# A two-layer encoder on one core: one more pair of the output projection by 7 products, two added transfers issued apart, and new numbers for the planner

## The chip, the cores and the metric

The kernel runs on one core of a Trainium2 chip. The metric is the device time of one execution in microseconds (us), the median of several runs. TensorE (PE in the profile) does the matmuls, VectorE (DVE) and ScalarE (ACT) the elementwise work, GpSimd (POOL) issues a part of the transfers and raises to powers, SyncE (SP) issues the loads of weights and the final stores.

## The reference

Two layers over 256 tokens of width 4096, all in float32. A layer normalises x, multiplies it by one combined matrix, runs grouped-query attention with axial rotary embedding and a two-way decayed retention on the parts, gates both, and adds the output projection to x:

```python
h = rmsnorm(x, norm_w[l])
proj = h @ w_in[l]                                  # 4096 x 11264
aq, ak, av, ag, rq, rk, rv, rg = jnp.split(proj, SPLIT_POINTS, axis=-1)
...
a_out = silu(ag) * gqa_attention(aq, ak, av)
r_out = silu(rg) * rmsnorm(bidirectional_retention(rq, rk, rv, ...), ret_norm[l])
x = x + jnp.concatenate([a_out, r_out], axis=-1) @ w_out[l]     # 4096 x 4096
```

A final normalisation with final_norm follows the second layer.

## The kernel before

**Blocks, pairs and products.** Each projection is computed in blocks of 2 x 512 output columns: 11 blocks of w_in and 4 blocks of w_out in each layer, 30 in all. A block sums over 4096 rows of the matrix, which are 32 tiles of 128, taken as 16 pairs (0 to 15). For one pair the work is a 2 x 2 by 2 x 2 product of tiles (two token tiles, two row tiles, two column halves). Plainly, that is 8 products of a 128 x 128 by a 128 x 512 tile. The pairs in SEVEN (0, 3, 6, 9, 12) do it with 7 products instead, after Strassen and Winograd: sums of x tiles and sums of weight tiles are made first, and seven results go into seven banks of PSUM, M1 to M7, which run over all pairs of the block. The other pairs do 8 products into four of the same banks (M2 to M5), using a third version of x (tile x3, the difference of two x tiles) so that their results fit the same final combination. In w_out the pairs in MORE take 7 products too. SEVENS holds both lists (for w_in, for w_out), EIGHTS the pairs that are in neither.

**Precision.** Every float32 value is split into a high part and a low part of the faster format float32r. A product is three matmuls: x high by weight high, x low by weight high, x high by weight low. In the profile these are the lines 1458 (high weights, two matmuls) and 1468 (low weights, one).

**Pages.** The weights of a pair come as two tiles of 128 x 2 x 512 (wraw, loaded by SP, 512 KB each) and are turned into pages, each a high part (whi, a copy on ACT) and a low part (wlo, a subtraction on DVE). A pair with 8 products has two pages, A and B, with 4 products each. A pair with 7 has four: A (M1, M3), T (M5, M7), B (M2, half a page), U (M6, M4); T and U are made of sums (wsum) that DVE computes first. RING = 5 pages are prepared ahead; a page that PE has used up lets the page five places on begin. The page B of the pairs in FAR_PAIRS (2, 5, 8, 11, 14) goes another way: ACT writes its high part and the negative of it (fhi, flo), and an adding transfer from POOL's queue makes the low part.

**Order.** GROUPS cuts the pairs into groups, each beginning with a pair of 7 products; pages_of lays the pages of the other pairs of a group between the four pages of its first pair. For w_out the groups are (0), (1,2), (3,4,5), (6,7,8), (9,10,11), (12,13,14,15). block (line 1347) makes the list of products, moves the product M7 of pair 0 to the second place, and sorts all products of pair 15 to the end in the order M3, M5, M4, M2 so that banks are finished one after another. combine (line 1475) empties a bank when its last product is issued: ACT copies M1, DVE adds the others into the tiles ca and cb (seven adds of 512 columns; M6 and M7 first).

**Last block.** Its order is M5, M2, M3, M4. The M4 products of the five pairs in DELAYED are left to the very end, so that the other banks can be finished, normalised and stored meanwhile. The halves of pages that these products need are kept in buffers of x whose pairs are done (dead_room, line 581, takes them in a fixed list). last_combine (line 1565) adds x, and finishes and stores the rows of the first token tile (row 0), then those of the second (row 1), eight stores of 256 KB each.

**Other work and the planner.** Attention, retention, the splitting of the next stage's x, and the tasks of a finished block are generators that are stepped while the program is built. The program keeps clocks of PE, DVE and ACT (Now, Clock) with assumed costs, and room (line 558) lets an optional step in only where weights would still be ready:

```python
low = 1.25 + 2 * PASS + MARGIN - rush[0]
...
max(ve.until, now.t) + STEP_V + low <= limit
and max(ac.until + STEP_S, free) + 1.05 + low <= end
```

PASS is 0.2; rush is 1.5 in the first block of w_out and 0 otherwise; limit and end are the times at which PE would reach the first page whose low part isn't issued, and the first page that isn't begun. LANDING, STORE, FETCH and FAR_LANDING are assumed times of transfers (a task that has issued one waits so long by the planner's clock before its next step). EARLY lets a task's next step come before its last operation is over. TIGHT_A and TIGHT_B are how many products at the start and the end of a block get a stricter test. The order in which instructions are issued is fixed when the program is built; on the chip the engines wait for each other by semaphores.

**After a block of w_out.** out_tasks (line 1558) adds the rows of x to the two finished tiles ca and cb by two adding transfers from POOL's queue, waits LANDING, and runs out_task for each: squares (ACT), a store of the new x, a transposition (DVE), a store or a move into place for the next layer. In the last layer it loads gains and multiplies by them instead.

## Time and profile before

| | |
|---|---|
| median of 3 runs | 2625.7 us (2624.82 to 2630.23) |
| the profiled execution, its own time | 2625.96 us |
| its span, from the first to the last instruction | 2623.8 us |
| granted TensorE clock, mean | 0.998 |
| DMA, mean over the span | 261 GB/s, of which HBM read 637.60 MB, written 44.04 MB |

How to read the rows: the engines are PE (TensorE matmuls), PEld (its weight loads, beside PE), DVE, ACT, POOL and SP; a name with q is an engine's queue of issued transfers. L1458 is line 1458 of the kernel; L247 is the helper through which all DVE and ACT operations are issued, so these are told apart by their tiles, written as out<-in. A row of a group gives the shapes, the count after x, then the busy time, the mean duration of one in ns, the idle time of the engine ahead of them, and what ended it. A row of waits gives who waited for whom: us in total, times, the longest. A row in order of time begins with the start and the duration in us; the idle time before it stands in brackets. Matmuls are pipelined: a row's duration (389 ns) is longer than the step from one to the next.

### The profile page before, as it was taken

Reading aid. Unit: us, or ns where it says so; the run is one execution under the profiler, and the core shown is the slowest. Engines: PE = TensorE matmul, PEld = TensorE weight load, DVE = VectorE, ACT = ScalarE, POOL = GpSimd, SP = SyncE. Lnnn points to the kernel's source line nnn. Section 1 sums busy time; section 2 is a strip of 40 time slices with the busy share of each in tenths; the row PEclk is TensorE's granted clock in tenths of the full one; section 3 lists DMA queues with packets and bytes.
Section 4 is the critical chain, followed back from the end, with each engine's and each line's share of the span. In section 5 each row is a group of like instructions: output and inputs, shape, how many; then the busy total and the mean of one; then the engine's idle time right before and its main releaser. Section 6 shows DMA issues by size and latency. Waiting matters only on the chain.

```text
span 2623.8 us, 34532 instructions
## 1 busy us (share of the span) xinstructions
PE 2601.0 (99%) x11725; PEld 2154.2 (82%) x11725; DVE 2166.6 (83%) x2684; ACT 1804.2 (69%) x2576; POOL 372.9 (14%) x510
## 2 busy tenths in 40 slices
PE   9999999999999999999999999999999999999998
PEld 7788888888888888888878888888888888888886
DVE  7898887798778898877978878888887688987876
ACT  8676676667565788655877666776576557876655
POOL 0012211221111101111111111211210111010000
PEclk9999999999999999999999999999999999999999
DMA  9988888887778777889988888888877787788887
GB/s 305 285 262 285 272 271 284 270 269 243 235 238 249 239 249 237 274 262 281 311 246 259 271 274 283 266 273 288 280 231 217 245 258 239 221 259 264 254 249 228
DMA packets 201121, 683.94 MB, mean 261 GB/s; under 512 B 24176, under 2 KB 30832, under 8 KB 200944
## 3 DMA queue, kind: packets, MB, share of 16 engines
q1 hardware_dynamic: 147760, 521.27, 56.3%
q0 software_dynamic: 53184, 160.46, 26.5%
q8 instruction: 92, 1.51, 0.2%
q14 instruction: 85, 0.70, 0.1%
HBM read 637.60 MB, written 44.04 MB: 260 GB/s over the span
## 4 chain that ended last, share of the span: by engine, by line
PE 92%; issue 1%; DMA 1%; ACT 1%; DVE 1%; POOL 0%; POOLq 0%; DVEq 0%; ACTq 0%
PE M L1458 59%; PE M L1468 30%; PE ps L973 1%; PE ps L974 1%; PE ps L975 1%; DMA q<-q_dram 1%; PE ps L1458 0%; DMA wraw<-in_w_in 0%; DVE wlo L247 0%; ACT ca L247 0%; DVE ca L247 0%; PE ps L1468 0%; DVE cb L247 0%; ACT pr L247 0%; ACT whi L247 0%
## 5 line engine op out<-in xcount | busy, mean ns | idle before, releaser
L247 ACT CAST whi<-wraw 128x1024 fp32r<-128x1024 f32 (+1 forms) x808 | 768.7, 962 | 463.0 <-PE M L1458 310.3
L247 DVE TENSOR_TENSOR wlo<-wraw,whi 128x1024 fp32r<-128x1024 f32 (+1 forms) x808 | 886.9, 1110 | 236.6 <-ACT whi L247 230.9
L1458 PE MATMUL M<-whi,x8h 128*128 128x512 f32 x1340 | 521.9, 389 | 0.0
L1458 PE MATMUL M<-whi,x8l 128*128 128x512 f32 x1340 | 521.5, 389 | 0.0
L1458 PE MATMUL M<-whi,x7h 128*128 128x512 f32 x1265 | 493.9, 390 | 3.7 <-DVE ca L247 2.5
L1458 PE MATMUL M<-whi,x7l 128*128 128x512 f32 x1265 | 492.9, 390 | 0.0
L247 ACT CAST whi<-wsum 128x1024 fp32r<-128x1024 f32 x314 | 329.6, 1050 | 137.1 <-PE M L1458 93.8
L1468 PE MATMUL M<-wlo,x8h 128*128 128x512 f32 x1340 | 420.2, 389 | 0.0
L247 DVE TENSOR_TENSOR wlo<-wsum,whi 128x1024 fp32r<-128x1024 f32 x314 | 382.5, 1218 | 38.7 <-ACT whi L247 36.8
L1468 PE MATMUL M<-wlo,x7h 128*128 128x512 f32 x1265 | 407.8, 389 | 1.1 <-DVE wlo L247 1.1
L1458 PEld LDWEIGHTS M<-whi,x8h 128*128 128x128 f32 x1340 | 251.6, 188 | 51.7 <-issue 0.2
L1458 PEld LDWEIGHTS M<-whi,x8l 128*128 128x128 f32 x1340 | 251.6, 188 | 51.7 <-issue 0.2
L1468 PEld LDWEIGHTS M<-wlo,x8h 128*128 128x128 f32 x1340 | 251.2, 188 | 51.7
L1458 PEld LDWEIGHTS M<-whi,x7h 128*128 128x128 f32 x1265 | 237.8, 188 | 55.7 <-DVE ca L247 2.9
L1468 PEld LDWEIGHTS M<-wlo,x7h 128*128 128x128 f32 x1265 | 237.5, 188 | 50.5 <-DVE wlo L247 1.5
L1458 PEld LDWEIGHTS M<-whi,x7l 128*128 128x128 f32 x1265 | 238.0, 188 | 48.9
L1458 PE MATMUL M<-whi,x 128*128 128x512 f32 x840 | 258.9, 389 | 0.7 <-ACT whi L247 0.7
L505 POOL DMA_DIRECT2D flo<-in_w_in x108 | 97.3, 901 | 1044.4 <-ACT flo L247 1001.4
L247 ACT CAST fhi<-wraw 128x1024 fp32r<-128x1024 f32 (+1 forms) x148 | 154.7, 1045 | 99.8 <-PE M L1458 93.9
L247 DVE TENSOR_TENSOR wsum<-wraw 128x1024 f32<-128x1024 f32 x157 | 191.2, 1218 | 18.7 <-DMA wraw<-in_w_out 11.3
L1458 PEld LDWEIGHTS M<-whi,x 128*128 128x128 f32 x840 | 157.1, 188 | 32.9 <-ACT whi L247 1.1
L1458 PE MATMUL M<-fhi,x8h 128*128 128x512 f32 x440 | 171.3, 389 | 0.0
(301 smaller groups left out, 3282.9 us busy)
## 6 DMA issues: line engine op xcount, KB each, us to landing
wraw<-in_w_in SPq DMA_DIRECT2D x700, 512.0 KB, 5.0
wraw<-in_w_out SPq DMA_DIRECT2D x256, 512.0 KB, 5.2
flo<-in_w_in POOLq DMA_DIRECT2D x108, 512.0 KB, 7.9
flo<-in_w_out POOLq DMA_DIRECT2D x38, 512.0 KB, 8.8
full<-next_dram POOLq DMA_DIRECT2D x18, 512.0 KB, 7.7
p_dram<-room POOLq DMA_DIRECT2D x64, 128.0 KB, 4.6
pT<-p_dram POOLq DMA_DIRECT2D x16, 512.0 KB, 8.1
next_dram<-room POOLq DMA_DIRECT2D x40, 128.0 KB, 5.9
```

What stands on the lines that cost most here:

```text
L247: return call(out, *args, **kwargs)
L505: nc.gpsimd.dma_start(g.lo[h], g.src[0][:, h, :], accum_op=ALU.add)
L973: nc.tensor.matmul(out, a[0], b[0], start=start, stop=False)
L974: nc.tensor.matmul(out, a[0], b[1], start=False, stop=False)
L975: nc.tensor.matmul(out, a[1], b[0], start=False, stop=stop)
L1458: nc.tensor.matmul(acc[name], a[i], g.hi[h], start=m == first[name] and not i, stop=False)
L1468: nc.tensor.matmul(acc[name], a, g.lo[h], start=False, stop=m == final[name])
```

## The change

Pair 13 joins pair 1 in MORE, so that in w_out it takes 7 products with four pages, and not 8 with two. From this follow: the groups of w_out become (0), (1,2), (3,4,5), (6,7,8), (9,10,11), (12), (13,14,15); EIGHTS has nine pairs; DELAYED becomes (8,10,11,14,15) where it was (10,11,13,14,15); one more buffer pair x7h, x7l is held, and one set of x8h, x8l, x3 less. dead_room takes its buffers in the order of the pairs instead of from a list. In out_tasks the second of the two adding transfers is issued a step of APART = 5.0 us of planner's time after the first; the first tile's task starts LANDING after the first issue as before, the second's not before LANDING after its own. Seven numbers of the planner are changed.

```diff
@@ -39,7 +39,7 @@
 RING = 5
 FAR = 1
 
-STEP_V = 1.6
+STEP_V = 0.7
 STEP_S = 1.3
 
 V_FIXED = 0.15
@@ -49,14 +49,14 @@
 PASS = 0.2
 
 LANDING = 11.0
-STORE = 8.0
-FETCH = 13.0
-FAR_LANDING = 11.0
-MARGIN = 0.0
+STORE = 6.0
+FETCH = 11.0
+FAR_LANDING = 13.0
+MARGIN = 0.6
 
 RUSH = 1.5
 
-EARLY = 0.7
+EARLY = 0.4
 
 ADD_AHEAD = 2.5
 
@@ -65,7 +65,7 @@
 PE_REST = 1.5
 
 TIGHT_A = 3
-TIGHT_B = 5
+TIGHT_B = 4
 
 AT_ONCE = 2
 
@@ -77,7 +77,7 @@
 
 SEVEN = (0, 3, 6, 9, 12)
 
-MORE = (1,)
+MORE = (1, 13)
 
 DELAYED = tuple([_p for _p in range(NP) if _p not in SEVEN + MORE][-5:])
 
@@ -211,6 +211,8 @@
 PLAIN_ORDER = ("M3", "M8", "M4", "M2")
 
 EASY = ("M7",)
+
+APART = 5.0
 
 TOGETHER = 4
 BANKS = ("M1", "M2", "M3", "M4", "M5", "M6", "M7", "M8")
@@ -589,8 +591,11 @@
                 "x7h": ("x7h", o, [P, 7, P], "p k t -> p (k t)"),
                 "x7l": ("x7l", o, [P, 7, P], "p k t -> p (k t)"),
             }
-            order = "x7h x7l x3 x3 x7h x7l x7h x7l x3 x8h x8l x7h x7l x3 x8h x8l x7h x7l x3 x7h" if MORE else "x3 x3 x8h x8l x3 x3 x8h x8l x7l x7h x3 x3 x8h x8l x3 x3 x8h x8l x7l x7h"
-            rooms.extend(kinds[v] for v in order.split())
+            for p in range(NP):
+                if p not in EIGHTS:
+                    rooms.extend(kinds[v] for v in ("x7h", "x7l"))
+                else:
+                    rooms.extend(kinds[v] for v in ("x3", "x8h", "x8l")[: 3 if p in EIGHTS[2:] and p not in DELAYED else 1])
         tag, bufs, shape, flat = rooms.pop(0)
         return t(ap, shape, tag, bufs, F32R).rearrange(flat)[:, :NB]
 
@@ -1558,9 +1563,13 @@
     def out_tasks(l, n, c):
         for i in range(2):
             nc.gpsimd.dma_start(c[i], residual(l, 2 * n + i), accum_op=ALU.add)
-        yield LANDING
-        for i in range(2):
-            yield from out_task(l, 2 * n + i, c[i])
+            if i < 1:
+                yield APART
+        second = now.t + LANDING
+        yield max(0.0, LANDING - APART)
+        yield from out_task(l, 2 * n, c[0])
+        yield max(0.0, second - now.t)
+        yield from out_task(l, 2 * n + 1, c[1])
 
     def last_combine(res):
```

## The prediction

> **What bounds the kernel now.** I read the page first (busy times, then the waits of TensorE), then the w_out stage block by block, because that is where the change removes work.
>
> ```profile
> span 2623.8 us, 34532 instructions
> ...
> PE 2601.0 (99%) x11725; PEld 2154.2 (82%) x11725; DVE 2166.6 (83%) x2684; ACT 1804.2 (69%) x2576; POOL 372.9 (14%) x510
> ...
> PE M L1468 <- DVE wlo L247: 2.8, 2, 1.7
> PE M L1458 <- DVE ca L247: 2.5, 3, 1.0
> PE ps L973 <- ACT pr L247: 2.0, 2, 1.0
> PE M L1458 <- DVE cb L247: 1.2, 1, 1.2
> PE ps L1671 <- DVE junk L247: 1.1, 1, 1.1
> PE M L1458 <- ACT whi L247: 0.7, 1, 0.7
> PE M L1452 <- ACT full L247: 0.7, 1, 0.7
> ```
>
> PE (TensorE) is busy 99% of the span, and all its listed waits together come to 11.0 us. The kernel is a queue of matmuls with almost no holes; time goes down by as many matmuls as are taken out, and up by any hole that is made. The row with junk and the one with full are the start, which the change leaves alone; 9.2 us of waits lie in the body.
>
> The blocks of w_out (one block is 1024 output columns), from windows cut where one block's first matmul starts to the next one's; columns are length, then busy time and instructions of PE, PEld, DVE, ACT, POOL, the granted clock, DMA share and GB/s:
>
> ```profile
> 978.30:1064.40 86.10, 86.10 (x392) 71.55 (x391) 77.43 (x104) 70.01 (x112) 8.14 (x8) 1.00 0.74 231
> ...
> 1230.40:1313.40 83.00, 83.00 (x367) 68.73 (x367) 76.95 (x111) 69.18 (x114) 14.66 (x21) 1.00 0.92 302
> ...
> 2363.30:2446.30 83.00, 83.00 (x368) 68.72 (x367) 64.50 (x68) 50.51 (x59) 6.09 (x7) 1.00 0.85 260
> ```
>
> DVE is the second engine: 77.43 of 86.10 us in layer 0's first w_out block, 76.95 of 83.00 in its last, but only 64.50 of 83.00 in a quiet one. So the cover for new DVE work is 6 to 18 us a block.
>
> **The change, part by part.**
>
> *Pair 13 with 7 products.* A product is three matmuls. Eight blocks of w_out (four in each layer) lose one product each: 8 x 3 = 24 matmuls. One step of the queue, from rows of single matmuls near the end (twelve steps between the last two of these):
>
> ```profile
> 2598.84 0.62 PE L1468 MATMUL M<-wlo,x7h 128*128 128x512 f32 x2
> ...
> 2609.27 0.39 PE L1468 MATMUL M<-x7h,x8h 128*128 128x512 f32 x1
> ...
> 2611.99 0.39 PE L1468 MATMUL M<-x7h,x8h 128*128 128x512 f32 x1
> ```
>
> (2611.99 - 2609.27) / 12 = 0.2267 us, so 24 x 0.2267 = 5.44 us leave the queue. That is the one sure term: **-5.44**.
>
> What it adds is weight preparation:
>
> ```profile
> L247 DVE TENSOR_TENSOR wlo<-wraw,whi 128x1024 fp32r<-128x1024 f32 x643 | 781.9, 1219 | 226.5 <-ACT whi L247 221.3 <-PE M L1458 2.4 <-PE M L1468 0.9
> ...
> L247 DVE TENSOR_TENSOR wlo<-wsum,whi 128x1024 fp32r<-128x1024 f32 x314 | 382.5, 1218 | 38.7 <-ACT whi L247 36.8 <-PE M L1468 1.5
> L247 ACT CAST whi<-wsum 128x1024 fp32r<-128x1024 f32 x314 | 329.6, 1050 | 137.1 <-PE M L1458 93.8 <-DVE wsum L247 37.0 <-PE M L1468 5.1
> ...
> L247 DVE TENSOR_TENSOR wsum<-wraw 128x1024 f32<-128x1024 f32 x157 | 191.2, 1218 | 18.7 <-DMA wraw<-in_w_out 11.3 <-DMA wraw<-in_w_in 7.4
> ...
> L247 DVE TENSOR_TENSOR wlo<-wraw,whi 128x512 fp32r<-128x512 f32 x165 | 113.0, 685 | 10.1 <-ACT whi L247 9.6 <-issue 0.2
> L247 DVE TENSOR_TENSOR wsum<-wsum,wraw 128x512 f32<-128x512 f32 x157 | 108.7, 692 | 5.5
> L247 DVE TENSOR_TENSOR wsum<-wraw,wsum 128x512 f32<-128x512 f32 x157 | 107.4, 684 | 0.1
> L247 ACT CAST whi<-wraw 128x512 fp32r<-128x512 f32 x165 | 102.0, 618 | 54.1 <-PE M L1458 46.9 <-DMA wraw<-in_w_out 6.7 <-ACT x L247 0.5
> ```
>
> A pair with 7 products costs DVE its sums (1.22 + 0.69 + 0.68) and the low parts of four pages (1.22, 1.22, 0.69, 1.22): 6.94 us. A pair with 8 costs two low parts, 2.44. So DVE gets 4.50 us more in each block, ACT 3 x 1.05 + 0.62 - 2 x 1.05 = 1.67 us. The same two weight tiles are loaded, so no DMA is added. In the quiet block DVE goes to 69.0 of 82.3 us: hidden. In layer 0's first block it is 81.9 of 85.4, in its last 81.5 of 82.3: hidden only if nothing is out of place. The added work of splitting x for pair 13 (once per layer) is a few DVE operations under 1 us and goes with this.
>
> *The order at the end of a block.* The groups were (12,13,14,15) and become (12) and (13,14,15). Products of pair 15 are sorted to the end, so the bank M6 used to get its last product in 12's page U, then came 14's page B (12 matmuls) and pair 15 (24 matmuls): 36 x 0.2267 = 8.16 us to the next block. Now it gets it in 13's page U, with only pair 15 behind it: 5.44 us. DVE therefore has 2.72 us less for the adds that empty the banks before the next block writes into them. The last 8.2 us of layer 0's four blocks:
>
> ```profile
> 1056.10:1064.40 8.30, 8.30 (x39) 6.86 (x38) 8.23 (x12) 4.34 (x5) 0.89 (x1) 1.00 0.84 260
> 1139.10:1147.30 8.20, 8.20 (x37) 6.78 (x37) 8.13 (x12) 4.38 (x5) 0.85 (x1) 1.00 0.61 163
> 1222.20:1230.40 8.20, 8.20 (x38) 6.80 (x37) 5.31 (x8) 3.27 (x4) 1.96 (x3) 1.00 0.79 229
> 1305.20:1313.40 8.20, 8.20 (x37) 6.77 (x37) 8.06 (x15) 5.52 (x7) 0.89 (x1) 1.00 0.61 214
> ```
>
> In the third, DVE is idle for 2.9 us, more than the 2.72 taken: no cost. In the other three it has about 0.1 us. Their cost is between 0 (the planner moves other DVE work out of the way) and 2.72 us each. I take a quarter, 0.7, as five weight pages are prepared ahead and PE showed no wait at any of these three: 3 x 0.7 = **+2.1**. Bounds for all seven ends that have a block behind them: 0 and 19.0.
>
> *The end of the kernel.* The same shift happens in the last block, where M6's adds start a chain that ends in the stores of row 0. There 14's page B has 9 matmuls ahead of the sorted ones, so the chain starts 9 x 0.2267 = 2.04 us later against the last matmul. Rows of DVE's and SP's orders of time, and one window of 2 us:
>
> ```profile
> 2599.57 0.69 DVE L247 TENSOR_TENSOR x7h<-wraw,x 128x512 fp32r<-128x512 f32 x1 [3.63 <-PE M L1468]
> 2600.18 0.68 DVE L247 TENSOR_TENSOR cb<-ca,M 128x512 f32<-128x512 f32 x1
> ...
> 2610.62 0.74 DVE L247 SCALAR_TENSOR_TENSOR cb<-cb,last,fn 128x512 f32<-128x512 f32 x1
> 2612.42 0.69 DVE L247 TENSOR_TENSOR ca<-ca,M 128x512 f32<-128x512 f32 x1 [1.05 <-PE M L1468]
> ...
> 2609.52 0.34 SPq L1618 DMA_DIRECT2D out<-ca  x1
> ...
> 2615.72 0.33 SPq L1618 DMA_DIRECT2D out<-ca  x1
> ...
> 2612.00:2614.00 2.00, 0.38 (x2) 0.00 (x0) 0.74 (x2) 0.72 (x2) 0.00 (x0) 1.00 1.02 379
> ```
>
> M6 is complete at about 2599.4 (its low matmuls start at 2598.84), and its add starts at 2600.18, behind a low part that waited for pair 12's buffer. After, the last such buffer is pair 10's x3, dead long before, so 0.6 us of the shift comes back: 1.4. Eight stores of 262 KB at 379 GB/s take 8 x 0.69 = 5.5 us; row 0's first is issued at 2609.52, row 1's at 2615.72, so there are 6.2 - 5.5 = 0.7 us of slack before row 1 queues behind row 0. The end moves by 1.4 - 0.7 = **+0.7** (0 to 1.4).
>
> *The two residual transfers apart.*
>
> ```profile
> ca<-in_x POOLq DMA_DIRECT2D x4, 512.0 KB, 7.1
> cb<-in_x POOLq DMA_DIRECT2D x4, 512.0 KB, 10.5
> ```
>
> The first tile's task starts 11 us after its issue as before, and the second's only when the first's is through. Issued 5 us later and landing 7.1 after that, the second is there at 12.1; were it wanted at 11, that would cost 1.1 us a time, but the first tile's squares, store and transposition stand in front of it. On POOL's queue, behind the second transfer, nothing moves but low parts of far pages, which get in between sooner. **0**.
>
> *The planner's numbers.* No instruction costs more or less by them; they decide when optional work is let in. DVE must show STEP_V + 1.65 + MARGIN of slack: 3.25 before, 2.95 after; ACT 4.0 before, 4.6 after (low parts and casts of weights come first more often). EARLY 0.4 queues less behind an unfinished operand. FAR_LANDING 13 and TIGHT_B 4 change only how long optional work is held back around far pages and a block's last products; they are taken with these. STORE and FETCH let the attention use q and P 4 us earlier, which speaks against the change, by the view of the tile q (us waited, times):
>
> ```profile
>   DMA q<-q_dram: 10.2, 4
> ...
> DMA to landing us min/median/max: 5.7/11.3/14.0
> ```
>
> ACT already waited 10.2 us for q, and PE's waits at the attention's ps behind it were 2.0 us, so 0.2 us of PE per us of ACT; eight groups by 4 us earlier would give at most 32 x 0.2 = 6.4 us lost. In the other direction, all 9.2 us of waits in the body could go, and with them a slow stretch:
>
> ```profile
> 98.40:101.90 3.50, 3.50 (x10) 2.75 (x9) 3.50 (x5) 2.54 (x6) 0.00 (x0) 0.53 1.04 268
> ```
>
> Ten matmuls in 3.5 us there, at a granted clock of 0.53, behind two of the waits: some 1.2 us lost. So -10.4 to +6.4; I take **-2.2**, a fifth of the gain end, since stricter ACT and EARLY act on most of the waits and only q's on the loss.
>
> The Trainium skill, "TensorE: Matmul & The Clock Gate", section "What's actually happening", says that an idle window of some 3.4 us puts the array on half clock until a busy window has passed; this trace agrees as to the 0.53, but it came after two short waits. By that rule each new hole could cost up to 1.7 us more, an estimate from the page; five such would make the slow rival below 2640. In the trace only one of the waits had it, so the sum is without.
>
> **Sum**, against the profiled execution's own 2625.96 us (2623.8 is its span): -5.44 + 2.1 + 0.7 + 0 - 2.2 = -4.8, so 2621.1. That execution stood 0.26 above the median of the runs, so **2620.9**; its own range, with ends of blocks between 0 and 5 and the planner within 3, is 2617 to 2625.
>
> **Rivals.**
> (1) *The planner's numbers remove DVE's waits at the starts of blocks*: the rows wlo, ca, cb, whi (7.2 us) and the slow stretch (1.2) go, 8.4 in place of 2.2: 2614.7. For it: all these waits follow DVE queues that hold optional work. Against: DVE's bar got lower, not higher.
> (2) *Slower: DVE becomes the bound at the ends of w_out blocks.* M7's bank is wanted by the next block's second product, three matmuls (0.68 us) in, so a full DVE costs 2.72 - 0.68 = 2.04 us. Paid at five ends it is 10.2: 2625.7 - 5.44 + 0.7 + 10.2 = 2631.2. It decides from 0.95 us an end. For it: 8.06 to 8.23 of 8.2 us busy; against: no wait there so far, and pages prepared far ahead.
> (3) *The gain is given back in the attention*: half of the 6.4, 3.2 in place of -2.2: 2626.3. For it: q landed late four times of eight; against: layer 1's PE hardly waited.
>
> **Chances**: forecast 0.40, (1) 0.24, (2) 0.19, (3) 0.17. A change of 0.2% (5.3 us) is about what a measurement of this kernel can tell from none. Half of the forecast and nearly all of (1) lie below 2620.4: faster 0.43. Half of (2) lies above 2631: with tails, slower 0.16. Same 0.41. The range takes in (3), most of (1) and half of (2): 2613 to 2632.
>
> **What would show it.** PE must count 24 matmuls fewer at a step still near 0.227. The last matmul would then lie some 5 us earlier and the stretch behind it be 0.7 us longer. The operations that make the sums rise from 157 to 165 each, low parts from sums from 314 to 330. New PE waits for DVE ca, cb or wlo near the starts of w_out blocks mean (2); more ACT waits for q, (3); PE waits below 6 us in the body, (1). The forecast fails if waits in the body change by more than 5 us either way, and its reasoning fails if DVE's share in w_out blocks does not rise by about 4.5 us.

## The result and the profile after

The changed kernel takes 2641.5 us (median of 5 runs, 2633.91 to 2643.5), against 2624.82 for the kernel before in the same session (5 runs): ratio 1.0055, 95% interval [1.0034, 1.0075]. (Ratios, here and below, are worked out over all runs of both kernels, so they are not quite the quotient of the two medians.) The forecast was 2620.9 with a range from 2613 to 2632; the time went the other way and out of the range.

The page of the changed kernel, its head and its busy times:

```profile
span 2639.7 us, 34559 instructions
...
PE 2601.6 (99%) x11701; PEld 2152.8 (82%) x11701; DVE 2200.9 (83%) x2727; ACT 1820.3 (69%) x2593; POOL 365.6 (14%) x511
```

PE issues exactly 24 matmuls fewer (11725 before), yet the span is 15.9 us longer. That PE's busy time stays is no contradiction: a matmul counts as busy for longer when it runs at half clock (0.63 us in the row at 1052.29 below, where 0.39 is usual). The sums rose as forecast, from 157 to 165 and from 314 to 330 (rows by group of the page; the lines of the code have moved, 1463 is now the high weights, 1473 the low ones, 249 the helper):

```profile
L249 DVE TENSOR_TENSOR wlo<-wsum,whi 128x1024 fp32r<-128x1024 f32 x330 | 401.5, 1218 | 47.1 <-ACT whi L249 46.9
...
L249 DVE TENSOR_TENSOR wsum<-wraw 128x1024 f32<-128x1024 f32 x165 | 200.6, 1216 | 21.4 <-DMA wraw<-in_w_out 13.0
```

PE's waits (us in total, times, the longest):

```profile
PE M L1473 <- DVE wlo L249: 10.1, 8, 5.2
PE M L1463 <- DVE x L249: 4.3, 2, 2.4
PE M L1463 <- DVE ca L249: 3.9, 4, 1.5
PE M L1473 <- DMA flo<-in_w_out: 2.5, 2, 1.8
...
PE M L1473 <- DMA x8h<-in_w_out: 1.2, 1, 1.2
```

Two kinds are new: x, and adding transfers of weights (flo, x8h; of these three waits two are in the last block, one in layer 0's last w_out block). The waits for wlo went from 2.8 to 10.1 us. Where the waits are is read from windows cut at the blocks' first matmuls (length, then busy time and count of PE, PEld, DVE, ACT, POOL, clock, DMA share, GB/s): the first and last w_out blocks of layer 0, the first and second of layer 1.

```profile
973.90:1066.20 92.30, 87.91 (x388) 71.88 (x388) 83.75 (x113) 68.93 (x107) 6.47 (x8) 0.98 0.73 222
1230.80:1316.60 85.80, 83.13 (x364) 67.89 (x363) 76.77 (x110) 68.69 (x113) 14.65 (x21) 1.00 0.89 286
2283.20:2374.50 91.30, 87.60 (x388) 71.90 (x387) 83.30 (x112) 68.99 (x107) 6.01 (x7) 0.98 0.72 222
2374.50:2457.10 82.60, 82.55 (x364) 68.04 (x363) 67.75 (x73) 51.70 (x60) 6.08 (x7) 1.00 0.82 253
```

The quiet block is what the forecast wanted everywhere: 82.6 where it was 83.0, with DVE up by 3.25 us (64.50 to 67.75) and hidden. A w_out block without a hole lasts 82.3 us now (82.96 less three steps of 0.2267), and the first one of a layer, which holds more, 85.1. What a block lasts beyond that I call its holes. They are worked out the same way for all blocks, and hold the waits and the slower matmuls behind them. (The first block of all counts 6.6 us both times, since its first 32 matmuls take 0.43 us each; it is in the last row alone.)

| holes, us | before | after |
|---|---|---|
| layer 0, w_in blocks 2 to 6 (the attention is in these) | 11.0 | 6.4 |
| layer 0, first w_out block | 0.2 | 7.2 |
| layer 0, last w_out block | 0 | 3.6 |
| layer 1, first w_in block | 4.6 | 8.3 |
| layer 1, first w_out block | 1.2 | 6.2 |
| layer 1, last w_out block | 0 | 5.4 |
| all 30 blocks | 25.5 | 45.8 |

So 20.2 us of holes came in and 5.44 us of matmuls went out. Three places explain most of it. The 3.6 us of layer 0's last w_out block are three more waits: 0.80 for a low part of pair 5, 0.75 for the far page of pair 8 and 1.13 for a low part of pair 13's page A.

*Pair 14 in the first w_out blocks.* PE's and DVE's orders of time in the changed kernel:

```profile
1050.40 0.50 PE L1463 MATMUL M<-whi,x 128*128 128x512 f32 x1 [2.42 <-DVE x L249]
...
1052.29 0.63 PE L1473 MATMUL M<-wlo,x 128*128 128x512 f32 x1
```

```profile
1046.01 0.69 DVE L249 TENSOR_TENSOR wsum<-wsum,wraw 128x512 f32<-128x512 f32 x1
1046.93 1.23 DVE L249 TENSOR_TENSOR wlo<-wraw,whi 128x1024 fp32r<-128x1024 f32 x1 [0.23 <-ACT whi L249]
1048.19 1.22 DVE L249 TENSOR_TENSOR wlo<-wsum,whi 128x1024 fp32r<-128x1024 f32 x1
1049.33 0.68 DVE L249 TENSOR_TENSOR wlo<-wraw,whi 128x512 fp32r<-128x512 f32 x1
1049.93 0.42 DVE L249 TENSOR_TENSOR x<-ca,x 128x256 fp32r<-128x256 f32 x1
```

The low part of pair 14's third operand (x<-ca) takes 0.42 us, but three low parts of weights stand ahead of it without a gap; two of them are pair 13's new pages T (made from a sum, wsum) and B. PE idles 2.42 us for it, from 1047.98 on. The queue is not all of that: ACT's high part of the same operand is itself done only at 1048.98, 1.0 us after PE began to wait.

```profile
1048.58 0.40 ACT L249 CAST x<-ca 128x256 fp32r<-128x256 f32 x1
```

In the kernel before, DVE stood idle for this operand, the low parts of weights came behind it, and it was done at 1051.14, 1.2 us ahead of the second of the two matmuls that want it:

```profile
1050.72 0.42 DVE L247 TENSOR_TENSOR x<-ca,x 128x256 fp32r<-128x256 f32 x1 [0.82 <-ACT x L247]
1051.07 1.22 DVE L247 TENSOR_TENSOR wlo<-wraw,whi 128x1024 fp32r<-128x1024 f32 x1
...
1052.11 0.62 PE L1458 MATMUL M<-whi,x 128*128 128x512 f32 x2
```

The change itself also wants the operand sooner: by the order of pages the matmul that waits is the 28th behind pair 12's first, where it was the 40th, and 12 x 0.2267 = 2.7 us. The wait and the slower matmuls behind it make some 4.2 of the 7.2 us of this block and 3.7 of the 6.2 in layer 1. Much of the rest is a wait for a bank add near the block's start (DVE ca, 1.46 and 1.27 us) and one for a low part (0.5 each), which e1_numbers below has as well, without pair 13.

*Page T at the start of layer 1.* First before, then after, DVE's order of time; the rows with M empty banks of the block that has just ended, the row wlo<-wsum is the low part that the new block's second product wants:

```profile
1310.20 0.68 DVE L247 TENSOR_TENSOR cb<-ca,M 128x512 f32<-128x512 f32 x1
1310.92 0.69 DVE L247 TENSOR_TENSOR ca<-cb,M 128x512 f32<-128x512 f32 x1
1311.52 0.68 DVE L247 TENSOR_TENSOR wsum<-wraw,wsum 128x512 f32<-128x512 f32 x1
...
1312.85 1.22 DVE L247 TENSOR_TENSOR wlo<-wsum,whi 128x1024 fp32r<-128x1024 f32 x1
```

```profile
1316.44 0.68 DVE L249 TENSOR_TENSOR cb<-ca,M 128x512 f32<-128x512 f32 x1
1317.15 0.69 DVE L249 TENSOR_TENSOR ca<-cb,M 128x512 f32<-128x512 f32 x1
1317.76 1.22 DVE L249 TENSOR_TENSOR wlo<-wraw,whi 128x1024 fp32r<-128x1024 f32 x1
1318.89 0.68 DVE L249 TENSOR_TENSOR cb<-cb,M 128x512 f32<-128x512 f32 x1
...
1322.61 1.22 DVE L249 TENSOR_TENSOR wlo<-wsum,whi 128x1024 fp32r<-128x1024 f32 x1
```

```profile
1323.88 0.79 PE L1473 MATMUL M<-wlo,x7h 128*128 128x512 f32 x1 [5.19 <-DVE wlo L249]
```

Before, the first bank add stood 3.2 us ahead of the new block (1313.4) and only two adds stood ahead of the sums. Now it starts 0.2 us ahead of the block (1316.6), six adds and a low part stand ahead of the sums, and page T's low part is 9.8 us later than before, in a block that starts 3.2 us later.

*The last block.* PE waits for the low part of a far page and for a kept half of one, both brought by adding transfers:

```profile
2598.76 0.50 PE L1473 MATMUL M<-flo,x8h 128*128 128x512 f32 x1 [1.76 <-DMA flo<-in_w_out]
...
2600.67 0.50 PE L1473 MATMUL M<-x8h 128*128 128x512 f32 x1 [1.18 <-DMA x8h<-in_w_out]
```

### The profile page after: what moved, and what is told of

Its sections match the earlier page's. It is cut to its first block, busy times and chain, and to the rows that moved or that the text cites. A ratio compares the mean times of both kernels' runs of the same rounds, so it can differ in the third digit from the quotient of the medians.

```text
span 2639.7 us, 34559 instructions
## 1 busy us (share of the span) xinstructions
PE 2601.6 (99%) x11701; PEld 2152.8 (82%) x11701; DVE 2200.9 (83%) x2727; ACT 1820.3 (69%) x2593; POOL 365.6 (14%) x511
## 4 chain that ended last, share of the span: by engine, by line
PE 86%; DMA 2%; DVE 2%; ACT 1%; issue 1%; POOL 0%; DVEq 0%; POOLq 0%; ACTq 0%; SPq 0%
PE M L1463 55%; PE M L1473 28%; DMA flo<-in_w_out 1%; PE ps L979 1%; PE ps L980 1%; PE ps L978 1%; DVE wlo L249 1%; DMA wraw<-in_w_out 1%; ACT whi L249 1%; DMA x8h<-in_w_out 0%; DVE wsum L249 0%; DVE ca L249 0%; DVE cb L249 0%; ACT fhi L249 0%; ACT ca L249 0%
## 5 line engine op out<-in xcount | busy, mean ns | idle before, releaser
L1463 PE MATMUL M<-whi,x7h 128*128 128x512 f32 x1493 | 584.1, 391 | 5.0 <-DVE ca L249 3.9
L1463 PE MATMUL M<-whi,x7l 128*128 128x512 f32 x1493 | 583.0, 390 | 0.0
L1473 PE MATMUL M<-wlo,x7h 128*128 128x512 f32 x1493 | 473.0, 390 | 9.3 <-DVE wlo L249 9.3
L1463 PE MATMUL M<-whi,x8h 128*128 128x512 f32 x1162 | 453.2, 390 | 0.0
L1463 PE MATMUL M<-whi,x8l 128*128 128x512 f32 x1162 | 453.2, 390 | 0.0
L1473 PE MATMUL M<-wlo,x8h 128*128 128x512 f32 x1162 | 364.4, 390 | 0.0
L1473 PEld LDWEIGHTS M<-wlo,x7h 128*128 128x128 f32 x1493 | 280.7, 188 | 70.6 <-DVE wlo L249 12.3
L1463 PEld LDWEIGHTS M<-whi,x7h 128*128 128x128 f32 x1493 | 281.6, 189 | 65.7 <-issue 3.5
L1463 PEld LDWEIGHTS M<-whi,x7l 128*128 128x128 f32 x1493 | 281.5, 189 | 58.0
L1463 PE MATMUL M<-fhi,x8l 128*128 128x512 f32 x438 | 170.4, 389 | 0.0
```

The costliest lines, as they stand in the source:

```text
L1463: nc.tensor.matmul(acc[name], a[i], g.hi[h], start=m == first[name] and not i, stop=False)
L1473: nc.tensor.matmul(acc[name], a, g.lo[h], start=False, stop=m == final[name])
```

## The experiments

Each run is compared with runs of the kernel before on the same chip. "Time" is the median, "before" that of these runs.

| run | what it is | time, us | before, us | ratio, 95% interval |
|---|---|---|---|---|
| e1_numbers | before + the seven numbers | 2626.35 | 2625.22 | 1.0003 [0.9994, 1.0013] |
| e2_pair13 | before + pair 13 | 2642.56 | 2625.22 | 1.0068 [1.0053, 1.0084] |
| e3_apart | before + transfers apart | 2627.18 | 2625.22 | 1.0007 [0.9998, 1.0017] |
| e4_no_apart | after, transfers together | 2637.33 | 2625.22 | 1.0045 [1.0030, 1.0060] |
| e5_pair4 | after, pair 4 for 13 | 2660.31 | 2623.14 | 1.0145 [1.0128, 1.0162] |
| e6_pair4_old | e2_pair13, pair 4 for 13 | 2649.61 | 2623.14 | 1.0104 [1.0089, 1.0119] |
| e7_whole13 | e2_pair13, 13's pages first | 2650.22 | 2623.14 | 1.0107 [1.0092, 1.0122] |
| e8_14b_behind | e2_pair13, 14's page B late | 2654.37 | 2623.14 | 1.0119 [1.0104, 1.0134] |
| e13_two_sums | e2_pair13, two splits at once | 2645.45 | 2627.92 | 1.0071 [1.0056, 1.0087] |
| e11_fetch_sooner | e2_pair13, x fetched sooner | 2658.31 | 2627.92 | 1.0122 [1.0107, 1.0137] |
| e12_before_sooner | before, x fetched sooner | 2651.75 | 2627.92 | 1.0096 [1.0081, 1.0111] |
| e10b_two_delayed7 | e13_two_sums, other delayed pairs | 2645.04 | 2627.92 | 1.0068 [1.0046, 1.0091] |
| e17_less_dve | after, less work on DVE | 2632.94 | 2626.65 | 1.0025 [1.0015, 1.0034] |
| e18_two_less_dve | e13_two_sums, less work on DVE | 2640.22 | 2626.65 | 1.0052 [1.0036, 1.0069] |
| e19_after_whole13 | after, 13's pages first | 2632.43 | 2626.65 | 1.0022 [1.0013, 1.0032] |
| e20_two_whole13 | e13_two_sums, 13's pages first | 2641.25 | 2626.65 | 1.0053 [1.0038, 1.0068] |
| e21_delayed7 | e19_after_whole13, other delayed pairs | 2633.07 | 2625.75 | 1.0036 [1.0022, 1.0050] |
| e21_delayed4 | e19_after_whole13, four delayed pairs | 2633.11 | 2625.75 | 1.0028 [1.0018, 1.0037] |

### The three parts, one at a time

The seven numbers on the kernel before; pair 13 with the new dead_room on the kernel before; the new out_tasks on the kernel before; and the changed kernel with the old out_tasks.

```diff
# e1_numbers, and the other six numbers
-STEP_V = 1.6
+STEP_V = 0.7
# e2_pair13, and the new dead_room
-MORE = (1,)
+MORE = (1, 13)
# e3_apart, and the rest of out_tasks; e4_no_apart takes the same out of the changed kernel
+            if i < 1:
+                yield APART
```

> The kernel before with the seven new numbers of the planner alone. Theory A (the place of pair 13 near the end of the block makes the loss): layer 0's w_in blocks gain as in the changed kernel (holes of its first six blocks 17.5 us before, 13.0 after), the first w_out blocks stay below 2 us of holes, so 2617 to 2624 us. Theory B (the numbers let too much work onto DVE in the loaded blocks): holes of 3 to 7 us in the first w_out blocks and in layer 0's last, 2630 to 2638 us.

> The kernel before with pair 13 by 7 products and the new list of buffers, old numbers, both transfers issued together. Theory A: holes of 4 to 8 us in each first w_out block as in the changed kernel, and layer 0's attention holes as before; 2636 to 2646 us. Theory B: 2619 to 2623 us, 24 matmuls fewer and holes as before.

> The kernel before with the two adding transfers issued 5 us apart and nothing else. If they cost nothing: 2622 to 2629 us with holes at the same places as before. Theory C (the second transfer's delay pushes the task of the second tile, its loads then collide with others): 2 to 5 us of new holes in layer 0's last block, at the start of layer 1 and in the kernel's last block; 2629 to 2634 us.

> The changed kernel with both adding transfers issued together again. Theory A and B: within 3 us of the changed kernel's 2641.5 (its holes in the first w_out blocks, 7.2 and 6.2 us, do not depend on it). Theory C: the holes in layer 0's last block (3.6), at the start of layer 1 (8.3) and in the last block (5.4) shrink by 5 us or more together; 2631 to 2636 us.

Pair 13 alone has the whole loss (+0.68%). The numbers alone and the transfers alone are not to be told from nothing. Taking the separation out of the changed kernel does not show either: the intervals with and without it overlap. The times of e1_numbers and e4_no_apart lie between the ranges that their theories gave. By the holes, the numbers do two things that cancel: in layer 0's w_in blocks 2 to 6 these fall from 11.0 to 6.7 us (in e2_pair13, on the old numbers, they are about 7 too, so not all of that need be the numbers), and in the first w_out blocks of both layers and layer 0's last one they rise from 1.4 to 7.1.

### Is it the place at the end of the block?

Pair 4 lies in the middle of a block and leaves the end as it was. Two runs take it in place of pair 13, with the new and the old numbers; two more keep pair 13 and change the order of the last group's pages.

```diff
# e5_pair4, e6_pair4_old
-MORE = (1, 13)
+MORE = (1, 4)
# in pages_of, with 13A for (13, PAGE_A) and so on: e7_whole13
+    if group == (13, 14, 15):
+        return [13A, 13T, 13B, 13U, 14A, 14B, 15A, 15B]
# e8_14b_behind
+    if group == (13, 14, 15):
+        return [13A, 14A, 13T, 13B, 13U, 14B, 15A, 15B]
```

> The changed kernel with pair 4 in place of pair 13 (new numbers, transfers apart). Theory A1: 2617 to 2624 us, with the holes of the first w_out blocks as in the kernel before with the new numbers (2.4 us each). Theory A2: 2630 to 2642 us.

> Pair 4 in place of pair 13 by 7 products, old numbers, transfers together: the same 24 matmuls less, the same work added on DVE and ACT in each block, but the last group stays (12,13,14,15). Theory A1 (the loss is in the place at the end of the block: pair 14's x is wanted earlier, and the adds of the banks come later against the block's end): holes in the first w_out blocks below 2 us, at the start of layer 1 below 4.6, none in the last block; 2619 to 2624 us. Theory A2 (the loss is DVE's extra 4.5 us in blocks that were already 90% full, wherever the pair lies): holes of 4 us or more in both first w_out blocks; 2632 to 2643 us.

> Pair 13 by 7 products, old numbers, transfers together, but its four pages in a row and pair 14 whole behind them: pair 14 starts 9.5 us after pair 12 does (8.8 before the change, 6.1 with pair 13 as it was changed), and the adds of M6 have 10.9 us to the block's end (8.2 before, 5.4 changed). Theory A1: the waits at pair 14 (0.9 us in each first block), the 4.7 us wait at the start of layer 1 and the flo waits of the last block go, 8 us or more; 2628 to 2635 us. Theory A2: DVE has 13.9 us of work for two such pairs in 9.5 us of matmuls, new waits for low parts in every w_out block; 2640 us or more.

> Pair 13 by 7 products, old numbers, transfers together, with 14's page B moved behind 13's page U: the adds of M6 have 8.2 us to the block's end again, but pair 14 still starts 6.1 us after pair 12. Theory A1: the 4.7 us wait at the start of layer 1 goes and the waits at pair 14 stay; 2635 to 2640 us. Theory A2: as with pair 13 alone, 2640 to 2645 us.

All four are slower than the kernel they vary. So the loss does not need pair 13's place at the end of the block: a further pair of 7 products in the middle costs more. But the place sets one wait. In e6_pair4_old, e7_whole13 and e8_14b_behind M6 is complete 8.2 us or more before the block's end, and the wait for page T in layer 1's first block is 1.5 to 1.7 us instead of 4.7 in e2_pair13 (and 5.2 in the changed kernel). That block as a whole gained nothing by it: its holes are 12.4 to 14.5 us, against 7.8 in e2_pair13, because near its end PE waits 5.2 to 5.9 us for x of pair 14. What these runs have in common is the wait for x: in e2_pair13, e7_whole13 and e8_14b_behind PE waits 4.5 us at pair 10 in the first w_out block of each layer, in e6_pair4_old 3.4 and 3.7, as in this row of e2_pair13:

```profile
1030.49 0.79 PE L1463 MATMUL M<-whi,x 128*128 128x512 f32 x1 [4.50 <-ACT x L249]
```

The x of pairs 10 and 11 is fetched there by a transfer on POOL's queue, which is issued only when few enough pages of memory are held. Before, and in e2_pair13:

```profile
997.02 0.76 POOL L786 DMA_DIRECT2D full<-next_dram  x1
```

```profile
1013.08 0.84 POOL L791 DMA_DIRECT2D full<-next_dram  x1
```

Sixteen microseconds later. DVE shows what was in between: pair 13's sums of x, for which pair 12's must be over first (a pair of 7 products splits its x alone), and which hold a page of their own and the page of pairs 12 and 13. Pair 12's last operation and pair 13's first in e2_pair13:

```profile
1008.40 0.82 DVE L249 TENSOR_TENSOR x7l<-xf,x7h 128x640 fp32r<-128x640 f32 x1
1009.13 0.29 DVE L249 TENSOR_TENSOR xf<-xf,ca 128x128 f32<-128x128 f32 x1
```

### Is it the page that pair 13's split holds?

Two pairs may be split at once; or x may be fetched with one page more in use, in the kernel with pair 13 and in the kernel before.

```diff
# e13_two_sums, in split_pair
-            while sums_of or held[0] + pledged() >= PAGES:
+            while len(sums_of) > 1 or held[0] + pledged() >= PAGES:
# e11_fetch_sooner, e12_before_sooner, the end of the condition in Turn.step
-held[0] + pledged() < PAGES - (2 if tasks else 0):
+held[0] + pledged() < PAGES - (1 if tasks else 0):
```

> Pair 13 with the old numbers (the kernel of 2642.56 us), and one condition relaxed: the splits of two pairs of 7 products may be under way at once, each with a page xf, so that pair 13's need not wait for the end of pair 12's. Theory of the page (the sixth seven pair of x hands back the page of pairs 12 and 13 late, so x of pairs 10 and 11 is fetched 16 us later than before, and TensorE waits for it 4.5 us at pair 10 of the first w_out block of both layers): by the planner's own clock that fetch moves from 1007.9 to 1000.0 us (997.5 in the kernel before), so the two waits of 4.5 us and the half-clock steps behind them go: 7 to 11 us less, 2631 to 2636. The waits at pair 14 (0.9), at page T of layer 1's first block (4.7) and for flo and x8h in the last block (1.8 and 0.9) stay. Theory of the sum (VectorE simply has 24 more operations, and what is not waited for at pair 10 is waited for elsewhere): the time stays at 2640 to 2645.

> Pair 13 with the old numbers, and x of a later chunk may be fetched while 7 of the 9 pages are held or promised instead of 6. By the planner's clock the fetch of pairs 10 and 11 moves from 1007.9 to 930.2 us, far ahead of its use. Theory of the page: the waits at pair 10 go (4.5 us in each layer with the steps at half clock behind them), as in the run with two splits at once; but one page less is left for sums and splits, which may put a wait at pair 14, as in the changed kernel (2.4 and 1.9 us), where the fetch is early too: 2632 to 2640. Theory of the sum: 2640 to 2645.

> The kernel before (no pair 13) with the same relaxed condition for fetching x. It has no wait for x at pair 10 to lose, so the theory of the page expects no gain: 2622 to 2630. If it is faster by more than 2 us, what the relaxed condition does to the run with pair 13 is not evidence for the page.

The theory of the page was right about the wait and wrong about the time. In e13_two_sums the wait at pair 10 is gone, and pair 14, 20 us further on, waits instead:

```profile
1050.77 0.49 PE L1463 MATMUL M<-whi,x 128*128 128x512 f32 x1 [1.01 <-ACT x L249]
1053.91 0.79 PE L1463 MATMUL M<-whi,x 128*128 128x512 f32 x1 [2.65 <-DVE x L249]
```

Fetching sooner is worse with pair 13 (9.2 us at pair 14, in both layers), and it makes the kernel before itself 1% slower (8.4 and 8.2 us there); both times are above every range given. A page taken early may be the one that is missing at pair 14 (that was not tried by itself); in any case one relief moves the wait.

### The amount of DVE's work, or the order?

Two runs leave out what pair 13's pages T and U add to DVE (their two low parts and the second sum, 3.8 us a block), while the planner still counts it, so order and loads stay. Two runs change the order only: all of pair 13's pages first, then 14's and 15's, so that pair 14 is wanted later and M6 is complete sooner.

```diff
# e17_less_dve on the changed kernel, e18_two_less_dve on e13_two_sums; for pair 13 alone
-                ve.tensor_add(self.u[:, 0, :], self.a[:, 1, :], self.v[:, 0, :])
-                ve.tensor_sub(self.u[:, 1, :], self.u[:, 0, :], self.b[:, 1, :])
+                self.u = self.v
# its pages T and U
-            lo = t(wp, [P, 2, NB], "wlo", RING, F32R)
+            lo = hi
# e19_after_whole13 on the changed kernel, e20_two_whole13 on e13_two_sums
+    if group == (13, 14, 15):
+        return [13A, 13T, 13B, 13U, 14A, 14B, 15A, 15B]
```

> The changed kernel with VectorE spared what pair 13's new pages cost: for its pages T and U the split's low part and the second sum are left out (32 VectorE operations over the 8 w_out blocks, about 3.8 us in each: 1.38 for the second sum, 2.44 for two low parts), so its products on these pages are wrong; the planner still counts the time, so order, loads and the number of matmuls stay as in the changed kernel. Theory of the sum (in the blocks where VectorE has no time left, 4.5 us more of it for 0.68 us less of TensorE turn into waits): the waits for wlo, ca and x at the first w_out blocks, at the end of layer 0 and at the start of layer 1 shrink to about those of the kernel before, and only flo and x8h in the last block stay: 2625 to 2632. Theory of the order (x of pair 14 is needed sooner, page T of the next block comes 2.7 us sooner after the last bank; the amount of VectorE's work is no matter): 2636 to 2642, the waits of 2.4 and 1.9 us at pair 14 and of 5.2 us at page T stay.

> The kernel with two splits of x at once (2645.45 us), with the same VectorE work left out. Theory of the sum: the waits at pair 14 (1.0 and 2.65 us in layer 0, 1.2 and 2.65 in layer 1) and at page T of layer 1 (4.6) go: 2629 to 2635. Theory of the order: pair 14 waits as before, 2641 to 2647.

> The changed kernel with the four pages of pair 13 first and then both of pair 14 and of pair 15 (13A 13T 13B 13U 14A 14B 15A 15B; it was 13A 14A 13T 14B 13B 13U 15A 15B). Pair 14 is needed 2 to 3 us later and bank M6 ends sooner before the block's end. Theory of the order: the waits for x at pair 14 (2.4 and 1.9 us with steps at half clock) and most of page T's 5.2 us go: 2628 to 2634. Theory of the sum: VectorE's work is the same, so other waits take their place: 2638 to 2648.

> Two splits of x at once with the old numbers, and the same order of pages as in the run before this. Theory of the order: no wait at pair 10 (x is fetched in time) and none at pair 14 (needed later): the holes of 7.5 and 7.2 us in the first w_out blocks fall under 2 and the time to 2630 to 2636. Theory of the sum: 2640 to 2650, with waits somewhere else in these blocks or in the block after.

Each of the two, alone, takes back 8 to 9 us of the changed kernel's loss (2641.5 to 2632.94 and 2632.43; by the ratios 0.30% and 0.33%). The first w_out block of layer 0, in e17_less_dve and in e19_after_whole13:

```profile
974.30:1063.50 89.20, 86.17 (x389) 70.81 (x388) 79.88 (x108) 69.04 (x108) 6.07 (x7) 1.00 0.75 227
```

```profile
974.30:1061.80 87.50, 85.70 (x388) 70.86 (x387) 80.66 (x108) 68.53 (x107) 6.07 (x7) 1.00 0.70 218
```

It lasted 92.3 us. With the work left out, the wait at pair 14 falls from 2.42 to 1.27 us and the clock stays at 1.00; with the new order that wait is gone, though DVE has all of its work, and PE's list of waits has no row for x at all:

```profile
PE M L1475 <- DVE wlo L251: 8.0, 10, 2.6
PE M L1465 <- DVE ca L251: 3.5, 4, 1.3
PE M L1475 <- DMA flo<-in_w_out: 3.2, 2, 2.3
```

So neither theory has the wait alone. With less work on DVE half of it stays, and there DVE's queue is no longer full. It is idle twice just ahead of the operand, waiting for ACT:

```profile
1046.41 1.23 DVE L249 TENSOR_TENSOR wlo<-wraw,whi 128x1024 fp32r<-128x1024 f32 x1 [1.55 <-ACT whi L249]
1048.18 0.69 DVE L249 TENSOR_TENSOR wlo<-wraw,whi 128x512 fp32r<-128x512 f32 x1 [0.55 <-ACT whi L249]
1048.79 0.42 DVE L249 TENSOR_TENSOR x<-ca,x 128x256 fp32r<-128x256 f32 x1
```

ACT's high part of the operand is done at 1048.45 in that run, PE waits from 1047.99. So what is left there is the order: it wants pair 14 2.7 us sooner than before, and ACT and DVE make the operand no sooner. A later want ends the wait; less work on DVE only shortens it.

e17 came out 0.9 us above what the theory of the sum gave, e19 inside what the theory of the order gave. On the old numbers the same edits show less: e18 is 5.2 us and e20 4.2 us under e13_two_sums, but the intervals overlap with its own, e18 lies 0.8 us under the range of the theory of the order, and e20 in that of the theory of the sum. Other waits remain or come: 2.0 us at pair 14 in both layers of e18_two_less_dve, and in e20_two_whole13 5.5 us for x at pair 14 of layer 1's first block, the wait that e6, e7 and e8 have as well. And the order of e19 is the one of e7_whole13, which made the kernel with pair 13 and the old numbers some 8 us slower. So this order helps in the changed kernel, not everywhere.

### The last block

With pair 13 at 7 products, pair 8 took its place in the list of delayed pairs, which became 8, 10, 11, 14, 15. Three runs take pair 8 out again, one on e13_two_sums and two on e19_after_whole13. (Two expectations give the changed kernel's list as 7, 8, 11, 14, 15, which is a slip: it holds 10, not 7.)

```diff
# e10b_two_delayed7, e21_delayed7
+DELAYED = (7, 10, 11, 14, 15)
# e21_delayed4
+DELAYED = (10, 11, 14, 15)
```

> The kernel with two splits at once, and the list of pairs whose last bank of the last block is delayed set to 7, 10, 11, 14, 15 instead of 7, 8, 11, 14, 15 (in the kernel before: 10, 11, 13, 14, 15; with 13 a seven, pair 8 and 7 came in). Theory: the waits for flo and x8h at pair 11 of the last block (1.75 and 0.89 us, with half-clock steps, 4.9 us in all) come from pair 8's late loads colliding with the residual's, so with pair 10 in its place they go: 3 to 5 us less than the kernel with two splits at once. Rival: the waits come from ScalarE being late with the last sums of 13 as such and stay: within 1.5 us of it.

> The changed kernel with all of pair 13 first in its group (2632.43 us), and pairs 7, 10, 11, 14, 15 instead of 7, 8, 11, 14, 15 as those whose last bank of the last block is delayed. Theory: pair 13 as a seven pushed pair 8 into this list, its two adding transfers stand 0.5 us apart amid the loads of the residual, and the holes of the last block (8.3 us with waits for flo 2.25, x8h 0.92 and x7l 0.62) come from that; with pair 10 they fall to 2 to 5 us and the time to 2626 to 2630. Rival: far loads at the end are late with any list: 2631 to 2634.

> The same kernel with four delayed pairs, 10, 11, 14 and 15, so one page B less is kept to the end and its four loads are ordinary ones. Theory: no adding transfer of pair 7 or 8 in the last block stands in the way, the flo and x8h waits go: 2624 to 2628, level with the kernel before (2626.65); 8 delayed matmuls fewer may put 0.5 to 2 us of waits for bank adds into the tail. Rival: 2631 to 2634.

None moves the time. The last block's holes are 3.9 us with the first (5.8 without), 5.5 and 4.0 with the others (8.3 without). In all three PE still waits for the low part of pair 11's far page and for its kept half (0.6 to 1.7 us each), in two of them for pair 8's far page as well (1.5 and 1.7), and the rest is spent elsewhere. That these holes come from the list alone is not borne out.

The traces show how near this was before. The second adding transfer of pair 11's page, in the kernel before and in the changed one:

```profile
2578.42 1.09 POOL L505 DMA_DIRECT2D x7l<-in_w_out  x1
```

```profile
2591.21 1.09 POOL L507 DMA_DIRECT2D x8h<-in_w_out  x1
```

Before, it is issued 49.2 us into the last block and takes 9.6 us, so it lands at 2588.0, and the matmul that wants it starts at 2588.19. In the changed kernel it is issued 51.8 us into the block and takes 9.4 us, and the matmul comes 6 matmuls (1.4 us) sooner, since pair 8's M4 products have moved to the end. The list of four pairs puts the matmul back, but not the issue (53.3 us into the block). A further pair of 7 products is not enough to bring this about: e6_pair4_old, where pair 8 is not delayed, issues it at 49.6 us and has no holes in this block. What makes the issue later was not tried, so the cause stays open.

No version with pair 13 beat the kernel before; the best that leaves nothing out, e19_after_whole13, is still 0.22% slower.

## Why the prediction was wrong, by its steps

**Matmuls, -5.44: right.** 24 fewer, and a block without holes is 0.68 us shorter, three steps of 0.2267.

**The covered work, costed at nothing: the step that failed.** The forecast had DVE's 4.5 us a block and the splitting of x "under 1 us and goes with this", "hidden only if nothing is out of place" in the first block, at 81.9 of 85.4 us. The work was sized well: DVE rose by 34.3 us over the span, 4.3 for each of the eight blocks. But a block's average is no cover. The quiet blocks hid it; the first ones did not, because there the same queues of ACT and DVE make operands of x with a time by which each is wanted. Pair 14's was 1.2 us early before and was 2.42 and 1.91 us late after, and the first w_out blocks have 12.0 us more of holes (7.2 + 6.2, less 0.2 and 1.2; the numbers alone, without pair 13, bring 3.4 of them). No operand of x was late there in the trace of before, and the forecast took that for room. It had also seen that the new order takes 2.72 us from the end of a block, but priced that for bank M6 alone: the same order wants pair 14's operand 2.7 us sooner, and that was no term of the sum. It also never asked what pair 13's split would hold: by itself (e2_pair13) that delayed the fetch of pairs 10 and 11 by 16 us and made waits of 4.5 us.

**The ends of w_out blocks, +2.1: right mechanism, wrong size and spread.** The ends of layer 0's first two w_out blocks, to which the forecast gave two thirds of its 2.1, cost nothing: the blocks behind them have no holes. At the one end that matters, into layer 1, the wait is 5.2 us where rival (2) had 2.04 as the most: it priced the bank M7 and overlooked page T's sums, which came to stand behind six bank adds and a low part instead of two adds. That block has 3.7 us more of holes than before, and layer 0's last block itself 3.6 (2.3 with the numbers alone). Orders in which M6 ends sooner had 1.1 to 2.1 us of wait there. The reading that PE showed no wait at any of these ends was wrong at this one: the kernel before waits there 1.00 us for a bank add, 4.8 us into layer 1's first block:

```profile
1318.25 0.50 PE L1458 MATMUL M<-whi,x7h 128*128 128x512 f32 x1 [1.00 <-DVE ca L247]
```

**The end of the kernel, +0.7: right** for what it counted: from the last matmul's start to the end of the span, 11.8 us became 12.8. But the last block's 5.4 us of holes, from the waits for flo and x8h, were no term of the sum: the adding transfers of kept halves were not costed, though one of them landed less than 0.2 us ahead of its use before.

**The transfers apart, 0: right** (1.0007 [0.9998, 1.0017] alone).

**The planner's numbers, -2.2: inside its bounds, but not paid.** Alone they gave 1.0003 [0.9994, 1.0013], so from 1.6 us less to 3.4 more. There is a gain of 4.6 us in layer 0's w_in blocks of the changed kernel, but not where rival (1) saw it. The starts of the second and third block keep their waits for wlo, cb and ca (holes 5.8 us before, 5.9 after); it is the three blocks behind them, with the attention, that lose theirs (5.3 and 0.7). Rival (3), q late in the attention, did not happen: no wait for ACT's pr or q's chain is in PE's list any more. The first and last w_out blocks give the gain back.

**The rivals.** (2) had the right engine and the wrong places: it gave 2631.2 for ends of blocks alone, 0.19 of chance, and against it counted that PE showed no wait there so far, which did not hold at the end into layer 1.

## What to carry to other kernels

When work moves onto an engine that is some 90% busy in a stage, ask of each dated result in its queue (an operand, a page to be freed, a bank add) how late it may come, and not how much idle time the stage has on average. Ask the same of the order: what is now wanted sooner, and who makes it. Where buffers, VectorE and ScalarE are all nearly full, taking away one wait moved it some 20 us on here; only a run shows whether the time follows. A change of order that lets the late result be wanted later was worth as much as taking the work away in the changed kernel, and cost some 8 us with the old numbers of the planner.

## What the runs showed of the hardware

A short idle time can put TensorE on half clock, and does so later than it occurs. In the changed kernel, the 2.42 us before pair 14 and what followed (windows):

```profile
1050.40:1051.90 1.50, 1.50 (x7) 1.24 (x7) 1.50 (x3) 0.96 (x2) 0.00 (x0) 1.00 1.02 221
1051.90:1055.90 4.00, 4.00 (x12) 3.17 (x11) 2.52 (x3) 1.21 (x2) 0.00 (x0) 0.57 1.02 367
1055.90:1059.90 4.00, 4.00 (x20) 3.27 (x19) 3.44 (x4) 2.71 (x3) 0.00 (x0) 1.00 0.59 210
```

Seven matmuls run at full clock, then for about 3.5 us the steps are 0.43 us, then 0.23 again: some eight matmuls at 0.2 more, 1.6 us on top of the wait. Behind 1.27 us at the same product (e17_less_dve) the clock stayed at 1.00. The Trainium skill, "TensorE: Matmul & The Clock Gate", section "What's actually happening", puts the array on half clock after an idle window of some 3.4 us that runs freely, until a busy one has passed. The length of the slow stretch agrees; the idle time that was enough, 2.42 us, is shorter than the page's window.

The length of a wait alone does not decide it. Layer 1's wait at the same product was 1.91 us in the changed kernel and 1.90 us in e4_no_apart; the 4 us behind them:

```profile
2358.70:2362.70 4.00, 3.98 (x10) 3.13 (x11) 2.57 (x3) 1.97 (x3) 0.00 (x0) 0.57 1.03 293
```

```profile
2358.40:2362.40 4.00, 4.00 (x17) 3.30 (x18) 3.53 (x4) 2.23 (x4) 0.00 (x0) 1.00 0.99 287
```

In all these runs every single wait of 2.2 us or more has such a stretch behind it, and between 1.8 and 2.2 us some have one and some have not; what decides there stays open. The stretch costs about 1 to 2.5 us each time. In the changed kernel the four of them make 6.3 us of the holes, where the kernel before has one of 1.5 us. The forecast had left this out of its sum, for only one place of the trace before had it.
